# The last FFN of a diffusion backbone: a first pair of eight direct products per weight, and another order of w2's seven products

## The chip, the cores and the metric

The kernel runs on one core of a Trainium2 chip. The metric is the device time of one execution in microseconds. A core has five instruction streams that matter here: TensorE (PE, matrix products into eight PSUM banks), VectorE (DVE), ScalarE (ACT), GpSimd (POOL), and SyncE (SP), which in this kernel issues the DMA transfers. Each stream runs its instructions in order.

## The reference, cut to what matters

The model has two layers; each ends with a SwiGLU FFN on 1024 latent tokens of width 1024. All that follows plays in the FFN of the last layer and the final norm:

```
h   = rms_norm(x, norm2_g) * (1 + ax2) + sx2
x   = x + gx2 * ((silu(h @ w1) * (h @ w3)) @ w2)
out = rms_norm(x, final_norm)
```

The hidden width is 22 blocks of 128, handled as 11 pairs of blocks.

## The kernel before

**Precision.** Every operand is split into a high and a low part (fp32r): ACT copies the high part (`split`, L177), DVE subtracts it to get the low part (L43). A product of two 128-wide operands is then three matmuls: high x high, high x low, low x high.

**Seven products.** Each product with a weight is a 2x2 block scheme with seven block products in place of eight (Strassen-Winograd). The two halves of 512 tokens are one index, the halves of the model width the other. `ops[0..6]` are the seven token operands: 0 and 5 are the two width halves of token half 0 (`b11`, `b21`), 1 and 3 come from half 1 (1 is `b12 - b11`, 3 is `b22`), and 2, 4, 6 are further sums. `WSet.get(i)` makes weight operand i of a pair: POOL builds a sum of raw weight blocks (into `fsum` or in place), ACT and DVE split it into a slot of `ring`. One product is 12 matmuls of 128x512 (L1412), into one of the PSUM banks A, B, C of its weight. `step(i)` in `Gate.seven` issues product i and what takes its result out of the bank; `gate` forms silu(h w1) * (h w3) of four blocks and seven sums of them, which go to DRAM (`g_d`) as the token operands of w2.

**The first pair.** Ahead of it runs the out-projection of the layer (`out_proj`, matmuls L215 to L217), half 0 and then half 1. Half 0 is normed and split as soon as it is there. Half 1's norm goes PE column (`pcol`, L160), DVE (`rsv`, L154), POOL (`rs`), PE broadcast (`prow`, L169), DVE (`nrm`, L46); only then can operands 1, 2, 3, 4, 6 be formed. In the first pair all four engines keep a hand-written order (L1969 and on): products 0 and 5 of w1 and w3, which need half 0 alone, then 1, 2, 3, 4, 6 of both. Five of the seven weight operands of the next pair's w1 (`n1`) are made here.

**Pairs 1 to 10** are ordered by a scheduler, products 0 to 6 of each weight in program order; DVE, ACT and POOL follow.

**w2.** Seven products i in `W2_ORDER`, each a loop over 11 steps j: `w2_op` loads and makes the weight operand, `x_op` loads the token operand from `g_d` and splits it, and four PSUM banks b take three matmuls each (L2053 to L2055). PE and SP keep the written order here, the others do not. Four banks are used over products 0 and 5, four others over 1 and 3, four over 2, 4 and 6. Behind the 11 steps of a product the results leave the banks by `put` (DVE, L46, into `xo`), partly with a saved copy of product 0 (`p1s`). `stat` squares a finished column on ACT into one of two `fsum` buffers and adds it up on POOL for the final norm; `col` and `scale` norm a finished half, and `scale` ends with its stores to `out` (L2088). The layer's input `xs_d` comes back into `xo` by loads at odd j of products 0, 5, 1, 3. The products 1, 3 and 2 share weight sums, kept in `stash`.

Of the kernel before, what the change touches and what calls it, by code (L numbers as in the profile page):

```python
# [8 lines left out]
F32 = mybir.dt.float32  # L9
# [26 lines left out]
def build(tc, a):  # L36
# [1307 lines left out]
    class WSet:  # L1344
        def __init__(self, f, n, j, place=False):
            self.f, self.s, self.place = f, [], place
            self.r = f.pre.pop(0) if f.pre else [f.raw(a[n][f.l, 2 * j + i]) for i in range(2)]
            self.w = {}

        def get(self, i):  # L1350
            if i not in self.w:
# [6 lines left out]
                elif i == 2:  # L1358
                    src = self.s[0] if self.place else self.f.fsum()
# [16 lines left out]
    class Gate:  # L1376
# [16 lines left out]
        def wset(self, n, j, place=False):  # L1393
            return WSet(self, n, j, place)

        def seven(self, w, o, done):
# [11 lines left out]
            def prod(n, i, start):  # L1408
                (wh, wl), (xh, xl) = w.get(i), self.ops[i]
# [6 lines left out]
            def step(i):  # L1416
# [3 lines left out]
                elif i == 1:  # L1420
                    v = prod("C", 1, True)
                    S.copy(out=tmp("p5"), in_=v)
                elif i == 2:
                    tt(V, o[0], st["p1"], prod("B", 2, True), ALU.add)
                elif i == 3:
                    tt(V, o[0], o[0], prod("C", 3, False), ALU.add)
# [10 lines left out]
            return step  # L1437

        def steps(self, store, ws):
# [5 lines left out]
            def gate(i, v):  # L1445
# [9 lines left out]
                if i == 2:  # L1455
                    store(5, b21)
                    tt(G, c[3], b21, c[4], ALU.subtract)
                    store(6, c[3])
                elif {0, 1, 3} <= have:
# [3 lines left out]
                    store(2, c[4])  # L1463

# [6 lines left out]
            return self.seven(ws[0], [s[:, i] for i in (1, 2, 3)], silu), self.seven(ws[1], c, gate), late  # L1471

        def pair(self, j, store, ws=(None, None), mid=None):
# [3 lines left out]
            for u in range(2):  # L1477
                for i in range(7):
                    ws[u].get(i)
                for i in range(7):  # L1480
# [4 lines left out]
    W2_ORDER = (0, 5, 1, 3, 2, 4, 6)  # L1485

    def w2_op(l, i, j, raw, fsum, slot, stash):
# [3 lines left out]
        if i == 2:  # L1491
            split(S, wh, wl, t)
            return wh, wl
        r = raw().rearrange("p (f k) c -> p f (k c)", f=2)
        if i in (0, 5, 6):
            q, c = {0: (0, 0), 5: (1, 0), 6: (1, 512)}[i]
            Q.dma_start(out=r[:, 0], in_=w[:, q, c:c + 512])
            src = r[:, 0]
        elif i == 1:
            Q.dma_start(out=r, in_=w[:, :, 512:])  # L1500
            tt(G, t, r[:, 0], r[:, 1], ALU.add)
            src = t
# [4 lines left out]
        else:  # L1507
            Q.dma_start(out=r, in_=w[:, :, 0:512])
            tt(G, t, t, r[:, 0], ALU.subtract)
            src = r[:, 1]  # L1510
            tt(G, src, src, t, ALU.subtract)
# [407 lines left out]
    first = [part(flat[i], 4)[:, c:c + 1024] for i in range(2) for c in (0, 1024)]  # L1919
# [11 lines left out]
    w1, w3 = [f.wset(n, 0, True) for n in ("ffn_w1", "ffn_w3")]  # L1931
    for w in (w1, w3):
        for i in (0, 5):
            w.get(i)
# [3 lines left out]
    for _ in range(2):  # L1938
        wr.tile([P, 4, P], F32, name="fsum", bufs=2)
    ring = [wr.tile([P, 1024], F32R, name=f"ring{i}") for i in range(4)]  # L1940
    for n, w, b in (("s", 2048, 1), ("pu", 512, 4)):
# [5 lines left out]
    t1, t3, late = f.steps(store(0), (w1, w3))  # L1947
    sh = lambda k: mod[:, 1, 3, 0, k:k + 1]

    def nrm(k):  # L1950
        stt(x[1][:, k], x[1][:, k], mod[:, 1, 4, 0, k:k + 1], pr, ALU.mult, ALU.mult)

    def bias(k):
        S.activation(out=x[1][:, k], in_=x[1][:, k], func=AF.Identity, bias=sh(k))

    def cutk(i, src, u, e=V):
        h, l, v = ops[i][0][:, kk[u]], ops[i][1][:, kk[u]], src[:, kk[u]]
        S.copy(out=h, in_=v)
        return lambda: tt(e, l, v, h.bitcast(F32), ALU.subtract)

    def subk(out, in0, in1):
# [306 lines left out]
```

## Time and profile before

| what | us |
|---|---|
| median of 3 runs | 3294.45 (3291.11 to 3295.41) |
| the profiled execution | 3295.82, its span 3294.0 |
| end of the out-projection, start of the first pair's own stretch | 2556.26 |
| first matmul of pair 1 | 2621.86 |
| first matmul of w2 | 3015.37 |
| last matmul of w2 | 3280.27 |

The span is the time from the first to the last instruction that the profiler saw; the execution's own time is 1.8 us longer. All later times are counted from the start of the span. PE is busy for 3057.9 us, 93% of the span, and its mean granted clock is 0.969 of full speed. The two stretches that the change touches begin at 2550: the first pair until about 2635, and w2 with the final norm from 3015 on.

### The profile page before, as it was taken

Reading aid. Unit: us, or ns where it says so; the run is one execution under the profiler, and the core shown is the slowest. Engines: PE = TensorE matmul, PEld = TensorE weight load, DVE = VectorE, ACT = ScalarE, POOL = GpSimd, SP = SyncE. Lnnn points to the kernel's source line nnn. Section 1 sums busy time; section 2 is a strip of 40 time slices with the busy share of each in tenths; the row PEclk is TensorE's granted clock in tenths of the full one; section 3 lists DMA queues with packets and bytes.
Section 4 is the critical chain, followed back from the end, with each engine's and each line's share of the span. In section 5 each row is a group of like instructions: output and inputs, shape, how many; then the busy total and the mean of one; then the engine's idle time right before and its main releaser. Section 6 shows DMA issues by size and latency. Waiting matters only on the chain.

```text
span 3294.0 us, 49782 instructions
## 1 busy us (share of the span) xinstructions
PE 3057.9 (93%) x18986; PEld 2730.4 (83%) x18986; DVE 2139.5 (65%) x3438; ACT 1323.2 (40%) x2649; POOL 1364.3 (41%) x1253
## 2 busy tenths in 40 slices
PE   6977999979999998999998999998999799999997
PEld 4656777769999998999998999998987588887775
DVE  5764777774876778777777466664355665555664
ACT  3324777553533334443434333321224333333433
POOL 1556881022744445454443332332122565552532
PEclk8998999989999999999999999999999899999998
DMA  7873001445433331433331101111125133324744
GB/s 243 267 169 101 16 19 46 123 132 198 148 109 116 110 109 65 160 111 108 109 114 72 46 27 38 39 43 45 39 78 201 45 115 99 105 97 155 261 155 139
DMA packets 167752, 360.21 MB, mean 109 GB/s; under 512 B 29513, under 2 KB 61913, under 8 KB 166745
## 3 DMA queue, kind: packets, MB, share of 16 engines
q1 hardware_dynamic: 167513, 357.03, 33.5%
q8 instruction: 149, 2.44, 0.3%
q14 instruction: 90, 0.74, 0.1%
HBM read 290.87 MB, written 66.10 MB: 108 GB/s over the span
## 4 chain that ended last, share of the span: by engine, by line
PE 66%; DVE 10%; issue 5%; ACT 4%; POOL 3%; DMA 2%; SPq 0%; POOLq 0%; DVEq 0%; ACTq 0%
PE psf L1412 11%; PE psf L1258 11%; PE psu L215 4%; PE psu L216 4%; PE psu L217 4%; PE psf L215 2%; PE psf L216 2%; PE psf L217 2%; PE pso L2053 2%; PE pso L2054 2%; PE pso L2055 2%; PE pso L217 2%; PE pso L216 2%; PE pso L215 2%; PE psl L1731 2%
## 5 line engine op out<-in xcount | busy, mean ns | idle before, releaser
L1412 PE MATMUL psf<-mix,ring 128*128 128x512 f32 x1320 | 321.6, 399 | 21.3 <-ACT ring L177 9.4
L215 PE MATMUL psu<-mh,wh 128*128 128x384 f32 (+1 forms) x1024 | 327.6, 320 | 1.7 <-ACT qr L1609 1.2
L217 PE MATMUL psu<-mh,wl 128*128 128x384 f32 (+1 forms) x1024 | 324.1, 317 | 0.0
L216 PE MATMUL psu<-ml,wh 128*128 128x384 f32 (+1 forms) x1024 | 323.4, 316 | 0.0
L1412 PEld LDWEIGHTS psf<-mix,ring 128*128 128x128 f32 x1320 | 251.2, 191 | 83.4 <-ACT ring L177 11.3
L215 PEld LDWEIGHTS psu<-mh,wh 128*128 128x128 f32 x1024 | 195.0, 190 | 2.2 <-ACT qr L1609 1.4
L43 POOL TENSOR_TENSOR fsum<-fraw,fsum 128x512 f32<-128x512 f32 x66 | 107.8, 1634 | 214.4 <-DVE ml L43 106.2
L216 PEld LDWEIGHTS psu<-ml,wh 128*128 128x128 f32 x1024 | 194.9, 190 | 0.1
L217 PEld LDWEIGHTS psu<-mh,wl 128*128 128x128 f32 x1024 | 194.7, 190 | 0.1
L46 DVE SCALAR_TENSOR_TENSOR x<-psf,mod,x 128x384 f32<-128x384 f32 (+1 forms) x352 | 175.4, 540 | 25.0 <-PE psf L217 21.1
L43 POOL TENSOR_TENSOR fsum<-fraw 128x512 f32<-128x512 f32 x77 | 117.2, 1523 | 106.2 <-DMA fraw<-ffn_w 94.3
L43 DVE TENSOR_TENSOR ml<-fraw,ml 128x512 fp32r<-128x512 f32 x132 | 124.3, 942 | 38.6 <-ACT ml L177 36.6
L43 POOL TENSOR_TENSOR s<-s,c 128x320 f32<-128x320 f32 x60 | 73.9, 1232 | 175.8 <-DVE c L43 167.1
L1258 PE MATMUL psf<-opx,mh 128*128 128x320 f32 x792 | 134.0, 310 | 0.8 <-DVE mh L43 0.8
L43 DVE TENSOR_TENSOR wx<-pT,wx 128x512 fp32r<-128x512 f32 x168 | 113.0, 681 | 33.4 <-ACT wx L836 33.4
L1258 PE MATMUL psf<-opx,ml 128*128 128x320 f32 x792 | 128.8, 310 | 0.2 <-DVE ml L43 0.2
L43 DVE TENSOR_TENSOR wl<-wraw,wh 128x1024 fp32r<-128x1024 f32 x61 | 90.4, 1481 | 59.2 <-ACT wh L177 49.1
L829 ACT ACTIVATE pt<-pss,st 128x512 f32<-128x512 f32 (+1 forms) x208 | 123.3, 603 | 13.4 <-DVE st L817 11.4
L43 POOL TENSOR_TENSOR acc<-acc,sq 128x384 f32<-128x384 f32 (+2 forms) x57 | 71.6, 1263 | 134.1 <-ACT sq L1129 120.2
L177 ACT CAST ml<-fraw 128x512 fp32r<-128x512 f32 x132 | 81.7, 619 | 113.0 <-PE psf L216 35.0
L43 POOL TENSOR_TENSOR xa<-xa,tot 128x1280 f32<-128x1280 f32 x24 | 87.2, 3632 | 90.4 <-ACT ku L1723 76.0
L1258 PEld LDWEIGHTS psf<-opx,mh 128*128 128x128 f32 x792 | 120.0, 188 | 3.5 <-issue 2.5
(457 smaller groups left out, 9213.5 us busy)
## 6 DMA issues: line engine op xcount, KB each, us to landing
fraw<-ffn_w SPq DMA_DIRECT2D x209, 512.0 KB
early<-w_mod SPq DMA_DIRECT2D x48, 512.0 KB
fraw<-w_mod SPq DMA_DIRECT2D x48, 512.0 KB
opx<-g_d SPq DMA_DIRECT2D x77, 256.0 KB
wraw<-w_odd SPq DMA_DIRECT2D x36, 512.0 KB
g_d<-s SPq DMA_DIRECT2D x44, 256.0 KB
g_d<-c SPq DMA_DIRECT2D x33, 256.0 KB
fraw<-ffn_w SPq DMA_DIRECT2D x33, 256.0 KB
```

What stands on the lines that cost most here:

```text
L43: return e.tensor_tensor(out=out, in0=in0, in1=in1, op=op)
L46: return V.scalar_tensor_tensor(out=out, in0=in0, scalar=scalar, in1=in1, op0=op0, op1=op1)
L177: S.copy(out=hi, in_=src)
L215: PE.matmul(ps, wh, xh, start=start, stop=False)
L216: PE.matmul(ps, wh, xl, start=False, stop=False)
L217: PE.matmul(ps, wl, xh, start=False, stop=stop)
L829: S.activation(out=o, in_=ps, func=AF.Exp, bias=st, accum_out=dd)
L1258: PE.matmul(ps, u[:, k], v[:, k], start=start and k == 0 and j == 0, stop=(k == 3 and j == 2), skip_group_check=True)
L1412: PE.matmul(ps(n), u[:, k], v[:, k], start=start and k == 0 and j == 0, stop=(k == 3 and j == 2), skip_group_check=True)
L1731: PE.matmul(ps[:, c], ku[:, c], qu, start=True, stop=True)
L2053: PE.matmul(o, wh, h, start=first, stop=False, skip_group_check=True)
L2054: PE.matmul(o, wh, l, start=False, stop=False, skip_group_check=True)
```

## The change

**First pair.** In place of seven products on sums, each weight makes eight direct products: its four raw blocks (weights 0, 5, 7, 6, with no sums) with operands 0 and 5 for half 0 and with operands 1 and 3 for half 1 (operand 1 is `b12 - b11`, so the half-1 banks hold a difference to half 0, and `eight` adds the half-0 result back). The eight products of half 0 of both weights come first. Operands 2, 4, 6 are formed for pair 1 only. PE alone keeps a hand-written order. The next pair's weights are no longer made there; `first`, w1's four slots, moves to the place of operand 2.

**Pairs 1 to 10** issue products 0, 5, 1, 3, 2, 4, 6 in place of 0 to 6. The stores of the last pair's seven sums are kept back and issued on SP behind w2's loads of step 3.

**w2.** Order 0, 2, 5, 4, 1, 6, 3; products 2, 4, 6 use one group of four banks, 0, 5, 1, 3 the other, so that the groups alternate. Product 2 loads three raw blocks a step and makes the stash with two POOL sums; 1 and 3 load one block and make one sum each. The loads of `xs_d` stand at the last four steps of products 0, 2, 5, 4. The stores of the half that is done first (now half 0) are issued behind all loads of the last product.

```diff
@@ class WSet, class Gate
-                    src = {0: a11, 5: a12, 6: a22}[i]
+                    src = {0: a11, 5: a12, 6: a22, 7: a21}[i]
...
+            def eight(h, f, half):
+                n, r = "AB"[f] if h == 0 else "CD"[f], ((0, 5), (7, 6))[f]
+                if half == 0:
+                    v = prod(n, r[0], True, (0, 1)[h])
+                    if h == 0:
+                        S.copy(out=tmp("q%d" % f), in_=v)
+                    return
+                v = prod(n, r[1], False, (5, 3)[h])
+                if h == 0:
+                    done(2 * f, v)
+                else:
+                    q = st["q%d" % f]
+                    d = o[2 * f] if o else q
+                    tt(V, d, q, v, ALU.add)
+                    done(2 * f + 1, d)
+            return eight if direct else step
...
-                for i in range(7):
-                    (t1, t3)[u](i)
+                for i in ORDER:
+                    (t1, t3)[u](i)
...
-    W2_ORDER = (0, 5, 1, 3, 2, 4, 6)
+    ORDER = (0, 5, 1, 3, 2, 4, 6)
+    W2_ORDER = (0, 2, 5, 4, 1, 6, 3)
@@ def w2_op
+            if i == 1:
+                tt(G, src, src, t, ALU.add)
+            elif i == 3:
+                tt(G, src, src, t, ALU.subtract)
...
+            r2 = rr()
+            Q.dma_start(out=r.rearrange("p f c -> p (f c)"), in_=w[:, 0])
+            Q.dma_start(out=r2[:, 0], in_=w[:, 1, 512:])
+            tt(G, t, r[:, 1], r[:, 0], ALU.subtract)
+            tt(G, t, t, r2[:, 0], ALU.add)
+            src = t
@@ the first pair
-    first = [part(flat[i], 4)[:, c:c + 1024] for i in range(2) for c in (0, 1024)]
+    first = [part(flat[i], 1)[:, c:c + 1024] for i in range(2) for c in (0, 1024)]
...
+    with tc.manual_schedule(engines={PE.engine}):
+        t1(0, 0, 0)
         acc.col(0, pp)
+        t1(0, 0, 1)
         pr = acc.bc(0, pp)
+        for k in range(KT):
+            h = x[1][:, k]
+            stt(h, h, mod[:, 1, 4, 0, k:k + 1], pr, ALU.mult, ALU.mult)
+            if k < 4:
+                stt(h, h, sh(k), b11[:, k], ALU.add, ALU.subtract)
+            else:
+                S.activation(out=h, in_=h, func=AF.Identity, bias=sh(k))
+            if k == 3:
+                cut(1, b12)
+        cut(3, b22)
...
+        t1(0, 1, 0)
+        t1(0, 1, 1)
+        for i in range(2):
+            for v in range(2):
+                t3(0, i, v)
+        sub(b12, b22, b12)
+        for i in range(2):
+            for v in range(2):
+                t1(1, i, v)
+        cut(2, b12)
+        sub(b11, b12, b11)
+        cut(4, b11)
+        sub(b12, b21, b12)
+        cut(6, b12)
...
+        for i in range(2):
+            for v in range(2):
+                t3(1, i, v)
...
+    kept = []
+    f.pair(NF // 2 - 1, lambda i, v: kept.append((i, v)))
@@ w2
+    PUT = {2: (1,), 5: (0,), 4: (3,), 1: (3,), 6: (2,), 3: (1,)}
+    P1 = {2: 1, 4: 3, 1: 2}
+    LOAD = {0: 1, 2: 0, 5: 3, 4: 2}
+    DONE = {5: 0, 1: 3, 6: 2}
...
+            ps = psb if i in (2, 4, 6) else psa
...
+                if i == 0 and j == 3:
+                    for u, v in kept:
+                        Q.dma_start(out=g_d[u, NJ - 1], in_=v)
+                if i in LOAD and j >= NJ - 4:
+                    d, t, _ = xv(LOAD[i], j - NJ + 4, 0, 0)
+                    Q.dma_start(out=xo[:, d, t:t + 512], in_=xs_d[t // 512, :, d, 0:512])
+                if not last or j < NJ - NT:
                     for b in range(4):
+                        mms(ps[b], *wx[j], b, 0, 512, new and j == 0, j == NJ - 1)
+                if last and j == 2:
+                    rs = col(0, 512)
+                if last and j == 4:
+                    out = scale(0, 512, rs)
+            if last:
+                out()
+                break
```

Three places in the instruction order. First PE, in the first pair, behind the broadcast of half 1's norm (`opx` holds operands 0 and 5 of half 0 and later of others, `mix` those of half 1; ring numbers name the weight slots, and the products before these rows are the same in both). Before:

```order
L1412 MATMUL psf<-opx,mix 128x512 x24
L1412 MATMUL psf<-mix,ring_24697 128x512 x12
L1412 MATMUL psf<-mix,ring_24698 128x512 x12
L1412 MATMUL psf<-mix,ring_24699 128x512 x12
L1412 MATMUL psf<-mix,ring_24697 128x512 x12
L1412 MATMUL psf<-mix,ring_24700 128x512 x12
L1412 MATMUL psf<-mix,ring_24698 128x512 x12
L1412 MATMUL psf<-mix,ring_24699 128x512 x12
L1412 MATMUL psf<-mix,ring_24700 128x512 x12
L1412 MATMUL psf<-mix,ring_24697 128x512 x12
```

And after:

```order
L1412 MATMUL psf<-opx,mix 128x512 x24
L1412 MATMUL psf<-opx,ring_24695 128x512 x12
L1412 MATMUL psf<-opx,ring_24696 128x512 x12
L1412 MATMUL psf<-opx,ring_24697 128x512 x12
L1412 MATMUL psf<-opx,ring_24698 128x512 x12
L1412 MATMUL psf<-mix 128x512 x48
L1412 MATMUL psf<-mix,ring_24695 128x512 x12
L1412 MATMUL psf<-mix,ring_24696 128x512 x12
L1412 MATMUL psf<-mix,ring_24697 128x512 x12
L1412 MATMUL psf<-mix,ring_24698 128x512 x12
```

Behind the broadcast 24 matmuls on half 0 followed before, then the products with half 1; now 72 on half 0 follow, then 96 on half 1.

Second SP, around the start of w2 (`g_d<-s` and `g_d<-c` are stores of the last pair's sums, `fraw<-ffn_w` and `opx<-g_d` the loads of a step's weight and token operand, `xo<-xs_d` the loads of the layer's input). Before:

```order
L2047 DMA opx<-g_d 128x512
L1497 DMA fraw<-ffn_w 128x512
L2047 DMA opx<-g_d 128x512
L1946 DMA g_d<-s 128x512 x2
L1946 DMA g_d<-c 128x512
L1946 DMA g_d<-s 128x512 x2
L1946 DMA g_d<-c 128x512 x2
L2110 DMA xo<-xs_d 128x512
L1497 DMA fraw<-ffn_w 128x512
L2047 DMA opx<-g_d 128x512
L1497 DMA fraw<-ffn_w 128x512
L2047 DMA opx<-g_d 128x512
```

And after:

```order
L1515 DMA fraw<-ffn_w 128x512
L2027 DMA opx<-g_d 128x512
L1515 DMA fraw<-ffn_w 128x512
L2027 DMA opx<-g_d 128x512
L2092 DMA g_d<-s 128x512 x2
L2092 DMA g_d<-c 128x512
L2092 DMA g_d<-s 128x512
L2092 DMA g_d<-c 128x512
L2092 DMA g_d<-s 128x512
L2092 DMA g_d<-c 128x512
L1515 DMA fraw<-ffn_w 128x512
L2027 DMA opx<-g_d 128x512
```

The seven stores stood behind two steps of loads and stand behind four now, and the first `xo` load, which came with step 1, follows at step 7.

Third POOL, in w2, where product 4 makes its weight sums (`fsum<-fraw`) and a finished column is added up (`sum...` or `acc...<-...,fsum`). Before, at the end of product 2:

```order
L43 TENSOR_TENSOR stash<-stash,fraw 128x512
L43 TENSOR_TENSOR fraw<-fraw,stash 128x512
L43 TENSOR_TENSOR sum_27638<-sum_27638,fsum 128x512 x2
L43 TENSOR_TENSOR fsum<-fraw 128x512
L43 TENSOR_TENSOR sum_27638<-sum_27638,fsum 128x512
L43 TENSOR_TENSOR fsum<-fraw 128x512 x10
L43 TENSOR_TENSOR sum_27638<-sum_27638,fsum 128x512 x4
```

And after, at the end of product 5:

```order
L43 TENSOR_TENSOR stash<-fraw 128x512
L43 TENSOR_TENSOR stash<-stash,fraw 128x512
L43 TENSOR_TENSOR acc_27628<-acc_27628,fsum 128x512 x3
L43 TENSOR_TENSOR fsum<-fraw 128x512 x11
L43 TENSOR_TENSOR fraw<-fraw,stash 128x512 x11
L43 TENSOR_TENSOR sum_27629<-sum_27629,fsum 128x512 x3
```

One of the sums of product 4 stood between the adds; now all three adds stand ahead of the eleven sums.

## Rows read from the trace of the kernel before

**Rows 1.** PE's waits, 2556 to 2660: engine, tile, line, releaser; total, times, longest us.

```profile
PE psf L1412 <- ACT ring L177: 9.4, 4, 4.7
PE psf L1412 <- ACT mix L1958: 6.3, 2, 6.1
```

**Rows 2.** Timeline of PE: start, duration, line, tile<-inputs, shape, count, [idle before <- releaser].

```profile
2530.38 0.39 PE L215 MATMUL pso<-mix,wh 128*128 128x512 f32 x1
...
2550.10 0.39 PE L215 MATMUL pso<-mix,wh 128*128 128x512 f32 x1
...
3036.98 0.39 PE L2053 MATMUL pso<-opx,mix 128*128 128x512 f32 x1
...
3046.78 0.39 PE L2053 MATMUL pso<-opx,mix 128*128 128x512 f32 x1
```

**Rows 3.** Windows: length, busy us (instructions) of each engine, granted clock, DMA share, GB/s.

```profile
2580.00:2590.00 10.00, 5.86 (x12) 3.76 (x12) 5.47 (x6) 4.40 (x5) 4.40 (x3) 0.51 0.00 0
...
2650.00:2800.00 150.00, 150.00 (x655) 122.58 (x654) 86.16 (x104) 50.21 (x87) 83.92 (x56) 1.00 0.32 108
...
3030.00:3040.00 10.00, 10.00 (x36) 7.93 (x35) 7.70 (x13) 7.02 (x12) 0.00 (x0) 0.79 1.05 386
```

**Rows 4.** Timeline of PE, end of pair 10 and w2.

```profile
3012.51 3.02 PE L1412 MATMUL psf<-mix,ring 128*128 128x512 f32 x12 [0.55 <-DVE c L43]
3015.37 0.39 PE L2053 MATMUL pso<-opx,ring 128*128 128x512 f32 x1
...
3028.63 0.79 PE L2053 MATMUL pso<-opx,ring 128*128 128x512 f32 x1 [7.16 <-ACT opx L177]
...
3198.42 0.80 PE L2053 MATMUL pso<-opx,mix 128*128 128x512 f32 x1 [4.41 <-ACT mix L177]
...
3257.81 0.79 PE L2053 MATMUL pso<-opx,mix 128*128 128x512 f32 x1 [12.32 <-ACT opx L177]
...
3280.27 0.28 PE L2055 MATMUL pso<-opx,mix 128*128 128x256 f32 x1
```

**Rows 5.** PE's waits for DVE's evictions, 3010 to 3294.

```profile
PE pso L2053 <- DVE xo L46: 9.8, 4, 4.0
```

**Rows 6.** Timeline of PE, first pair.

```profile
2556.26 2.26 PE L1412 MATMUL psf<-opx,mix 128*128 128x512 f32 x9
...
2559.76 3.03 PE L1412 MATMUL psf<-opx,mix 128*128 128x512 f32 x12
...
2563.45 3.05 PE L1412 MATMUL psf<-opx,mix 128*128 128x512 f32 x12
```

**Rows 7.** Timeline of DVE, first pair: a weight split, a normalisation, splits.

```profile
2560.02 0.68 DVE L43 TENSOR_TENSOR ring<-fsum,ring 128x512 fp32r<-128x512 f32 x1
2563.73 0.75 DVE L46 SCALAR_TENSOR_TENSOR x<-x,mod,prow 128x512 f32<-128x512 f32 x1 [3.03 <-PE prow L169]
...
2568.09 1.23 DVE L43 TENSOR_TENSOR mix<-x,mix 128x1024 fp32r<-128x1024 f32 x1
...
2579.93 2.28 DVE L43 TENSOR_TENSOR x<-x 128x1024 f32<-128x1024 f32 x1
```

**Rows 8.** Timeline of POOL, the norm's column.

```profile
2560.18 1.40 POOL L43 TENSOR_TENSOR rs<-rsv,nhalf 128x4 f32<-128x4 f32 x1 [5.73 <-DVE rsv L154]
```

**Rows 9.** Timeline of SP: DMA issues at w2's start and in its last product.

```profile
3013.08 1.89 SPq L1946 DMA_DIRECT2D g_d<-s  x2
...
3023.00 0.42 SPq L1497 DMA_DIRECT2D fraw<-ffn_w  x1
...
3247.64 3.49 SPq L2088 DMA_DIRECT2D out<-xo  x4
```

**Rows 10.** Timeline of POOL, product 3: first of the two sums of two steps.

```profile
3107.92 1.74 POOL L43 TENSOR_TENSOR stash<-stash,fraw 128x512 f32<-128x512 f32 x1
...
3111.33 1.74 POOL L43 TENSOR_TENSOR stash<-stash,fraw 128x512 f32<-128x512 f32 x1
```

**Rows 11.** Timeline of POOL, end of product 2: the first add of squares.

```profile
3192.13 1.30 POOL L43 TENSOR_TENSOR sum<-sum,fsum 128x512 f32<-128x512 f32 x1 [40.47 <-ACT fsum L2070]
```

More of the change, by code (lines that the diff above doesn't have):

```diff
@@ L1358, in get @@
                 elif i == 2:
[L1359 removed]
+                    src = self.f.fsum()
                     tt(G, src, self.s[0], a11, ALU.subtract)
@@ L1436, in step, with steps @@
                     done(2, o[1])
-            return step
-        def steps(self, store, ws):
+            def eight(h, f, half):
[14 more added lines that the diff above has]
+            return eight if direct else step
+        def steps(self, store, ws, direct=False):
             nh, have = self.nh, set()
@@ L1470, in late @@
                 c.extend(ct[:, i] for i in range(5))
-            return self.seven(ws[0], [s[:, i] for i in (1, 2, 3)], silu), self.seven(ws[1], c, gate), late
+            return (self.seven(ws[0], [s[:, i] for i in (1, 2, 3)], silu, direct),
+                    self.seven(ws[1], None if direct else c, gate, direct), late)
         def pair(self, j, store, ws=(None, None), mid=None):
@@ L1946, in build @@
     store = lambda j: lambda i, v: Q.dma_start(out=g_d[i, j], in_=v)
-    t1, t3, late = f.steps(store(0), (w1, w3))
+    t1, t3, late = f.steps(store(0), (w1, w3), True)
     sh = lambda k: mod[:, 1, 3, 0, k:k + 1]
[L1950 to L1959, printed above, removed]
@@ L2097, in build @@
                 ps = [bank() for _ in range(4)]
-            if i == 1:
-                stash = big.tile([P, KT * T], F32, name="stash", tag="H0")
-                wslots[0] = itertools.cycle(ring + [flat[0][:, c:c + 1024] for c in range(0, 10240, 1024)])
-            new, end = i in (0, 1, 2), i in (5, 3, 6)
-            u = DEST.get(i, 0)
+                if i == 2:
+                    psb, stash = ps, big.tile([P, KT * T], F32, name="stash", tag="H0")
+                else:
+                    psa = ps
@@ L2103, in build @@
+            ps = psb if i in (2, 4, 6) else psa
+            new, last = i in (0, 1, 2), i == W2_ORDER[-1]
             wx = [None] * NJ
             for j in range(NJ):
-                wx[j] = w2_op(1, i, j, fraw, fsum, next(wslots[0]), stash), x_op(i, j)
-                if i in (0, 5, 1, 3) and j % 2 and j < 8:
-                    q, d = divmod({0: 0, 5: 3, 1: 1, 3: 2}[i], 2)
-                    d = 4 * q + j // 2
-                    t = {0: 0, 5: 1, 1: 1, 3: 0}[i]
-                    Q.dma_start(out=xo[:, d, 512 * t:512 * t + 512], in_=xs_d[t, :, d, 0:512])
@@ new lines, in build @@
+                if last and j == 2:
[5 more added lines that the diff above has]
+                break
+            for b in range(4):
+                if i == 0:
+                    S.copy(out=p1s[:, b], in_=ps[b])
+                for u in PUT.get(i, ()):
+                    put(ps[b], *xv(u, b, 0, 512))
+                if i in P1:
+                    put(p1s[:, b], *xv(P1[i], b, 0, 512))
+                if i in DONE:
+                    stat(xv(DONE[i], b, 0, 0)[0], 512 * (DONE[i] % 2), 512)
@@ new lines, in build @@
+        for t0, n in (0, 256), (256, 256):
+            for b in range(4):
+                for j in range(NJ - NT, NJ):
+                    mms(ps[b][:, t0:t0 + n], *wx[j], b, t0, n, False, j == NJ - 1)
+                put(ps[b][:, t0:t0 + n], *xv(1, b, t0, n))
+                stat(b, 512 + t0, n, V if t0 else G)
+                if t0 and b == 1:
+                    rs = col(512, 256)
+                if t0 and b == 3:
+                    scale(512, 256, rs)()
+        scale(768, 256, col(768, 256))()
```

167 lines of the change are left out of this document (37 added, 130 removed).

## The prediction

> **What bounds the kernel now.** I read the waits of TensorE (PE) first, in the two stretches that the diff touches, then its timeline there, then the engines that end the waits, then SP's queue. In the first pair of the last FFN PE waits mostly for ScalarE's (ACT) copies, of half 1's operands (mix) and of weights (ring) [rows 1], and VectorE (DVE) and GpSimd (POOL) make what ACT copies. Where nothing is missing PE starts a 128x512 matmul every 0.2267 us: 87 of them lie between the two rows of [rows 2] (19.72 us). In w2 it is 42 matmuls in 9.80 us, 0.2333 us each. Pairs 1 to 10 leave PE no idle time: in 2650 to 2800 it is busy 150.00 of 150.00 at full granted clock [rows 3]. So a microsecond saved in front of them is a microsecond of the end, and one saved in w2 too, as long as the tail behind the last w2 matmul keeps its length.
>
> How much the two stretches lose now:
> - Pairs 1 to 10 are 10 x 14 x 12 = 1680 matmuls, 380.9 us at 0.2267. w2 starts at 3015.37 [rows 4], so without any loss pair 1 would have had to start at 2634.5. That is the effective end of the first pair.
> - w2 is 7 x 11 x 12 = 924 matmuls' worth, 215.6 us at 0.2333. From 3015.37 to the last matmul at 3280.27 it takes 264.9 [rows 4]. With about 3 us for the norm's small matmuls, some 46 us are lost. PE's waits of 7.16, 4.41 and 12.32 us [rows 4] and four for DVE's evictions, 9.8 us [rows 5], are 34 of them; the other 12 are matmuls at the lower clock behind them (granted 0.51 of full speed behind the like wait in the first pair [rows 3]).
>
> **The first pair.** Sixteen products for fourteen: 24 matmuls more, 5.4 us of PE. In return eight of them (96 matmuls, for four before) need half 0 alone, which is there before the out-projection ends. 3 of the 192 run ahead of 2556.26, so 189 x 0.2267 = 42.8 us. The norm's two small groups stand between the products as before and cost 1.46 us (2558.30, the end of the nine matmuls, to 2559.76) and 0.97 us (2562.48 to 2563.45) [rows 6]. PE alone would end at 2556.26 + 42.8 + 2.4 = 2601.5. Three things can be late:
> - Operands 1 and 3. The eight products of half 0 end at 2556.26 + 2.4 + 93 x 0.2267 = 2579.8. DVE's new order has eight normalisations and four subtractions of 0.75 us from 2563.73 on [rows 7], so until 2572.7, then three to four splits of 1.23 us alone, up to 2.28 when POOL runs beside them [rows 7]. Operand 1 is ready at 2575.2 to 2577.3, in time; operand 3, one product later (2582.5), at 2578.9 to 2584.1. Loss 0 to 1.6.
> - The norm's column rs on POOL. It started at 2560.18 [rows 8]; now three sums for pair 1 (1.3 us each) stand ahead of it, behind a load. If the load is there by 2556 rs moves to about 2560.5, which the next twelve matmuls cover; each us of a later load is a us of the first pair. Loss 0 to 3.
> - Pair 1's weights. w1's first slots now lie in operand 2's place, so operand 2 is split only when the w1 products end (2579.8 + 48 x 0.2267 = 2590.7), and ring2 lies where the half-1 input still is. Behind 2590.7 stand four to five DVE steps of 1.23 to 2.28: 2596 to 2602, with pair 1's splits behind, against 2601.5. Loss 0 to 8.
>
> I take 3 us for the three together: effective end 2604.5, gain 2634.5 - 2604.5 = **30 us**, between 21 and 33.
>
> The Trainium skill, "SBUF — State Buffer", section "Who interferes with whom", says that a DVE instruction with two SBUF inputs and a GpSimd instruction that reads SBUF exclude each other for the whole instruction. It speaks against the second POOL sum per step, below: The trace agrees for a single split, 1.23 us alone and 2.28 beside POOL [rows 7]. Taken strictly, product 2 would take 3.96 us a step by it where POOL and DVE did with 3.41 before [rows 10]; the sum would be 3242.
>
> **Pairs 1 to 10.** The order 0,5,1,3,2,4,6 puts three products of bank B next to each other in program order, each waiting for DVE's add of the one before. In the instruction order the other weight's products lie between them, 27 to 50 matmuls at the places I looked at. The only neighbours are at the end of pair 10, as before, where the wait is 0.55 us [rows 4]. I take 0.
>
> **w2.** Four losses of before and what is in their place:
> - Its start. Before, seven stores of the last pair, each waiting for its product, stand on SP ahead of the third step's loads: first store 3013.08, next weight load 3023.00 [rows 9], PE waits 7.16 us [rows 4] and is slow after. Now four steps of loads (4 x 2.8 us of PE work, until 3026.6 on the old time axis) come first, and the x_s loads have moved behind step 7. The last pair's last product ends with the start of w2 and the stores' data are there some us later, so the fifth step's load follows in time or nearly. Loss 1 (0 to 4); was about 10.
> - The bank waits. Products now alternate between two groups of four banks, so eviction has a whole product (30.8 us) of time: the four waits of [rows 5] go (about 16 us with the slow clock). Their price: product 2 makes its weights with two POOL sums a step. POOL with two sums a step ran at 3.41 us (3107.92 to 3111.33 [rows 10]) against PE's 2.8. Eleven steps are 37.5 us; POOL can start some 8 us before product 2 does, as loads of product 0 free buffers. 37.5 - 8 - 28 (PE's start of the eleventh step) = 1.5, and 512 + 256 KB of weights and 256 KB of x a step are 1 MB, 2.7 us at the 386 GB/s of [rows 3]. Raw buffers hold two steps only, so a slow landing adds. Loss 4 (0 to 10).
> - Product 4. Its weight sums use the two fsum buffers that the squares of the finished half-column use as well; before, PE waited 4.41 us there [rows 4]. Now three squares and adds of product 5, 1.30 us each [rows 11], stand ahead of the first sum on POOL. From the end of product 5: 0.2 until the first square is there, three adds, a sum of 1.6, a copy of 0.6 make 6.4 us, with 2.4 at the lower clock 9. Was 7. Loss 9 (6 to 12).
> - The last product. Before, the finished half's four stores held SP (the last wait and their issue end at 3247.64 + 3.49 = 3251.1 [rows 9], loads only then), PE waited 12.32 us [rows 4]: about 15 with the slow clock. Now stores are issued behind all loads: 0. The norm of that half comes in step 2 of the last product, and its adds on POOL alternate with that product's sums: loss 2 (0 to 4).
>
> 1 + 4 + 9 + 2 = 16 in place of 46: gain **30 us**, between 18 and 40. The tail behind the last matmul is the same code on the other half: 0.
>
> **The sum** is made against the profiled execution, 3295.82 us (span 3294.0): 3295.8 - 30 - 30 = 3235.8. It lies 1.4 us above the median, so I say 3235.
>
> **Rivals.**
> - The first pair is bound by its elementwise work. Only PE keeps a hand-written order there; before, all four engines had one. If all splits take 2.28 us and rs is late by 3, pair 1's weights come at 2612 to 2615 and the lower clock adds a few: gain 18 for 30, 3248. For it: DVE was busy most of the time there, and PE's present waits are all of this kind [rows 1]. Against it: half 0's products cover 2557 to 2580. 0.15.
> - w2 gives back more. If POOL and DVE shut each other out in product 2, a step takes its two POOL sums and two DVE splits one behind the other, 2 x 1.30 + 2 x 0.68 = 3.96 us [rows 7, 11]; 0.55 over 3.41 is 6 us in eleven steps; and if product 4 starts as late as the old last product did (12.32 us for 6.4), 6 more: 3248. For it: one split did take 2.28 for 1.23; against it: the 3.41 was measured with the same four steps. 0.12; both rivals at once, 3260, 0.04.
> - Slower: bank B. If PE reaches products 4 and 6 before DVE's add has freed their bank, in pairs 1 to 10 there are 2 waits x 2 weights x 10 pairs = 40 on a path that has no idle time now. At the 0.55 us of [rows 4] they cost 22; a DVE add caught behind a split of 2.28 makes it 2.4 us and 96 in all, 3332. It decides from 1.5 us each, where it eats the 60. Against it the interleaving above. 0.04.
> - The change does less than it says: the interleaving of loads keeps the start of w2 as it is (SP still held by a store that waits), +9, 3245. In the instruction order the loads do stand ahead. 0.05, inside the range.
>
> **Chances.** Forecast 0.60, first-pair rival 0.15, w2 rival 0.12, late start 0.05, both 0.04, slower 0.04. What a measurement of this kernel can tell from no change is about 0.2%, 6.6 us. Faster 0.94, within 0.02 (a mix of bank waits and lost gains), slower 0.04. The range goes from full gains (33 and 40: 3222, two less for the profile) to both rivals with a little over: 3220 to 3262.
>
> **What would show it.** In the new profile: the first w2 matmul some 30 us earlier, at 2985; waits for ACT mix in the first pair gone, waits for ACT ring under 4 us in all; no wait for DVE xo in w2; one wait of 6 us for ACT's copy in product 4; none in the last product. Wrong it would be if PE were under 10.00 busy in pairs 1 to 10 (bank B), if waits of over 8 us for ACT ring stood around the start of pair 1, or if product 2 showed a wait in every step.

## The result, and the profile after

The changed kernel (called after below) takes 3241.5 us (median of 4 runs, 3237.1 to 3254.1), the kernel before 3292.8 in the same runs: a ratio of 0.985, 95% interval 0.982 to 0.988. The forecast was 3235, with 3220 to 3262 as its range. The profiled execution of after has a span of 3242.6 us, 51.4 less than before.

Where they went is read from three stretches of PE's timeline. What runs ahead of them is the same code in every kernel here, but begins the last FFN up to 11.5 us earlier or later from run to run; so lengths are compared, not times of day: from the nine matmuls at the end of the out-projection to the first matmul of w2; from there to the last matmul of w2; and the tail to the end of the span.

| | first pair and pairs 1 to 10 | w2 | tail |
|---|---|---|---|
| before | 459.1 | 264.9 | 13.7 |
| after | 436.7 | 236.7 | 12.7 |
| forecast (before less its terms) | 429 | 235 | 13.7 |

PE's timeline of after in the first pair (start, duration, line, tile<-inputs, shape, count, idle before and its releaser):

```profile
2556.50 2.26 PE L1412 MATMUL psf<-opx,mix 128*128 128x512 f32 x9
...
2567.43 3.07 PE L1412 MATMUL psf<-opx,mix 128*128 128x512 f32 x12 [0.68 <-ACT pu L1443]
...
2574.85 5.86 PE L1412 MATMUL psf<-opx,ring 128*128 128x512 f32 x24 [1.55 <-ACT pu L1443]
2581.39 3.07 PE L1412 MATMUL psf<-opx,ring 128*128 128x512 f32 x12 [0.68 <-ACT pu L1443]
2584.30 11.06 PE L1412 MATMUL psf<-mix 128*128 128x512 f32 x48
2595.20 11.04 PE L1412 MATMUL psf<-mix,ring 128*128 128x512 f32 x48
2606.08 0.62 PE L1412 MATMUL psf<-opx,ring 128*128 128x512 f32 x2
```

Half 1's operands come in time: the 48 matmuls on `mix` start without a wait, where [rows 1] had 6.3 us of waits for ACT's copies of them, and the 9.4 us for its copies of weights have gone too. Three waits for ACT at L1443 stand there instead, each for the copy of a half-0 result out of its PSUM bank. The first of them stood in the kernel before as well, in PE's timeline at the same place; the other two are new:

```profile
2567.17 3.07 PE L1412 MATMUL psf<-opx,mix 128*128 128x512 f32 x12 [0.68 <-ACT pu L1419]
```

Pair 1 starts 49.6 us behind the nine matmuls.

Its w2, same view:

```profile
2990.28 3.04 PE L1412 MATMUL psf<-mix,ring 128*128 128x512 f32 x12 [0.78 <-DVE c L43]
2993.15 0.39 PE L2033 MATMUL pso<-opx,ring 128*128 128x512 f32 x1
...
3049.02 0.50 PE L2035 MATMUL pso<-opx,mix 128*128 128x512 f32 x1 [0.90 <-DVE mix L43]
...
3094.60 0.80 PE L2033 MATMUL pso<-opx,mix 128*128 128x512 f32 x1 [6.01 <-ACT mix L177]
...
3202.36 1.87 PE L160 MATMUL pcol<-onec,acc 128*128 128x2 f32 x8 [4.37 <-POOL acc L43]
...
3229.87 0.28 PE L2035 MATMUL pso<-opx,mix 128*128 128x256 f32 x1
```

The waits of [rows 4] at the start (7.16) and in the last product (12.32) and the four of [rows 5] have gone. Product 4 waits 6.01 us, product 2 in four places 1.8 us together (the largest is shown), and a wait of 4.37 us has come in front of the norm's column product (L160), which stands in PE's order behind step 2 of the last product.

### The profile page after: what moved, and what is told of

Read it like the earlier page. It is cut to its first block, busy times and chain, and to the rows that moved or that the text cites. A ratio compares the mean times of both kernels' runs of the same rounds, so it can differ in the third digit from the quotient of the medians.

```text
span 3242.6 us, 49888 instructions
## 1 busy us (share of the span) xinstructions
PE 3045.4 (94%) x19010; PEld 2727.4 (84%) x19010; DVE 2113.4 (65%) x3431; ACT 1321.8 (41%) x2643; POOL 1352.8 (42%) x1251
## 4 chain that ended last, share of the span: by engine, by line
PE 67%; DVE 8%; issue 5%; POOL 4%; ACT 4%; DMA 2%; SPq 0%; POOLq 0%; ACTq 0%; DVEq 0%
PE psf L1412 13%; PE psf L1258 11%; PE psu L215 5%; PE psu L216 5%; PE psu L217 5%; PE psf L215 2%; PE psf L216 2%; PE psf L217 2%; PE pso L217 2%; PE pso L216 2%; PE pso L215 2%; PE psl L1751 2%; PE pso L2033 2%; PE pso L2035 2%; PE pso L2034 2%
## 5 line engine op out<-in xcount | busy, mean ns | idle before, releaser
L1412 PE MATMUL psf<-mix,ring 128*128 128x512 f32 x1248 | 295.7, 392 | 0.8 <-DVE c L43 0.8
L1412 PEld LDWEIGHTS psf<-mix,ring 128*128 128x128 f32 x1248 | 234.4, 188 | 53.2 <-DVE c L43 1.2
L43 POOL TENSOR_TENSOR fsum<-fraw,fsum 128x512 f32<-128x512 f32 x64 | 99.7, 1558 | 234.1 <-DVE ml L43 105.3
L43 POOL TENSOR_TENSOR fsum<-fraw 128x512 f32<-128x512 f32 x75 | 108.1, 1442 | 130.8 <-DMA fraw<-ffn_w 99.7
L1412 PE MATMUL psf<-opx,ring 128*128 128x512 f32 x528 | 131.4, 393 | 2.2 <-ACT pu L1443 2.2
L829 ACT ACTIVATE pt<-pss,st 128x512 f32<-128x512 f32 (+1 forms) x208 | 123.5, 604 | 13.5 <-DVE st L817 11.5
```

What stands on the lines that cost most here:

```text
L43: return e.tensor_tensor(out=out, in0=in0, in1=in1, op=op)
L829: S.activation(out=o, in_=ps, func=AF.Exp, bias=st, accum_out=dd)
L1412: PE.matmul(ps(n), u[:, k], v[:, k], start=start and k == 0 and j == 0, stop=(k == 3 and j == 2), skip_group_check=True)
```

## What the experiments asked

Three losses in after had a suspected cause: the copies at L1443, the 6.01 us at product 4, and the 4.37 us. Parts of the change were taken back: w2 as a whole, the places of two sets of stores and of the loads of the layer's input, and the alternation of the bank groups. In what follows a stretch is one of the three lengths above.

## The first pair alone

w2 is the old one here; the first pair and the order of products in pairs 1 to 10 are the new ones.

```diff
-    W2_ORDER = (0, 2, 5, 4, 1, 6, 3)
+    W2_ORDER = (0, 5, 1, 3, 2, 4, 6)
...
-    f.pair(NF // 2 - 1, lambda i, v: kept.append((i, v)))
+    f.pair(NF // 2 - 1, store(NF // 2 - 1))
```

(w2_op and the loops of w2 as in the kernel before.)

> The new first pair and the new order of products in pairs 1 to 10, with w2 as it was before. Theory: the first pair is worth 22 us and w2 the rest, and the two are independent: w2 starts near 2993 as in the changed kernel and takes the old 265 us from there to its last matmul; time 22 us under the kernel before, ratio 0.993. Rival: part of the gain of the first pair was won at the cost of work pushed into w2 (or the reverse); then w2's length moves by 4 us or more from 265.

Measured: a ratio to the kernel before of 0.9935 (0.9921 to 0.995), 3270.8 us. The stretches are 436.6, 264.3 and 13.2. w2 has its old length and its old waits, PE's timeline:

```profile
3004.63 0.80 PE L2033 MATMUL pso<-opx,ring 128*128 128x512 f32 x1 [7.83 <-ACT opx L177]
...
3233.01 0.80 PE L2033 MATMUL pso<-opx,mix 128*128 128x512 f32 x1 [12.44 <-ACT opx L177]
```

The two halves of the change are independent, as expected: the first pair is worth 22 us, w2 the other 28. The new order of products in the pairs has no part in it: the 1344 matmuls of pairs 2 to 9 take 308.6 us in after and 308.8 before.

## The copies out of a shared bank

```diff
         t1(0, 0, 0)
         acc.col(0, pp)
-        t1(0, 0, 1)
+        t1(0, 1, 0)
...
-        t1(0, 1, 0)
+        t1(0, 0, 1)
         t1(0, 1, 1)
-        for i in range(2):
-            for v in range(2):
+        for v in range(2):
+            for i in range(2):
                 t3(0, i, v)
```

> The first pair's half-0 products in the order 0, 7, 5, 6 of each weight, so that the two products that share a PSUM bank no longer follow each other. Theory: the three waits for ACT's copy of the half-0 result (0.7, 1.6 and 0.7 us) come from that neighbourhood and vanish; pair 1 starts 2.9 to 3.5 us earlier against the end of the out-projection (46.1 to 46.7 us behind the nine matmuls, in place of 49.6), and the end moves by as much, some 3 us. Rival: ACT is late there in itself, behind the splits of half 1's operands; then the waits move to the second copies and the sum stays within 0.7 of 2.9 us.

Measured, PE's timeline (one execution; its time is 3240.1 us):

```profile
2554.69 2.26 PE L1412 MATMUL psf<-opx,mix 128*128 128x512 f32 x9
...
2600.55 0.62 PE L1412 MATMUL psf<-opx,ring 128*128 128x512 f32 x2
```

No wait stands between them; pair 1 starts 45.9 us behind the nine matmuls, 3.7 us earlier than in after, a little more than the waits' 2.9 since each had some tenths of refilling behind it. The stretch is 432.9 for 436.7. In after, the product that adds to a bank came right behind the one whose result ACT had to copy out of it first: 0.7 us when ACT is free (a copy takes 0.6), 1.55 when it was behind three splits. With a product of another bank between them there is nothing to wait for. w2, whose code is the same, came out 0.7 us longer than in after (237.5 for 236.7), so the net is 3.0 us, as expected; 0.7 is also a measure of what w2 differs by from one execution to the next.

## The start of w2: stores or loads

The change moved two things on SP at the start of w2: the last pair's stores, and the loads of the layer's input (`xo<-xs_d`). First the stores alone go back into the pair:

```diff
     kept = []
-    f.pair(NF // 2 - 1, lambda i, v: kept.append((i, v)))
+    f.pair(NF // 2 - 1, store(NF // 2 - 1))
```

> Only the place of the last pair's seven stores goes back: issued within the pair, ahead of w2's third or so step of loads. Theory: SP is held by them again, PE waits some 7 us for ACT's copy of a token operand soon after the start of w2, with 2.4 us at the lower clock behind it: 7 to 10 us slower than the changed kernel. Rival: the x_s loads, which stood at the odd steps before and now stand behind step 7, were what held SP; then the wait stays under 3 us.

Measured: no wait at the start of w2 at all; stretches 438.3, 232.9 and 12.2, in sum 2.7 us shorter than after (w2 3.8 and the tail 0.5 shorter, the end of pair 10 with 1.4 us more of waits). But the edit didn't bring the stores early, as SP's timeline of this run shows:

```profile
2979.82 0.38 SPq L1515 DMA_DIRECT2D fraw<-ffn_w  x1
...
2984.36 0.42 SPq L2027 DMA_DIRECT2D opx<-g_d  x1
2993.68 0.32 SPq L1963 DMA_DIRECT2D g_d<-s  x1
...
2998.14 1.70 SPq L1963 DMA_DIRECT2D g_d<-c  x2
3001.65 0.32 SPq L2095 DMA_DIRECT2D xo<-xs_d  x1
```

and of after:

```profile
2972.04 0.42 SPq L2027 DMA_DIRECT2D opx<-g_d  x1
2981.97 10.75 SPq L2092 DMA_DIRECT2D g_d<-s  x2
...
2998.65 0.40 SPq L1515 DMA_DIRECT2D fraw<-ffn_w  x1
```

Left to the scheduler, six of the seven stores went out behind the loads of eight steps, just ahead of the first load of `xs_d` behind step 7. That is later than in after, where the stores that are kept behind step 3 hold SP from 2972 to 2998 with only four steps loaded. So the run doesn't test the theory; it shows what the stores cost behind step 3. What they delay is not the start but product 2: its first weight sum on POOL starts at 3016.35 in after, 23.2 us behind the start of w2, and at 3014.15 here, 19.8 behind it, and its four waits are gone. So the second suspect went back as well:

```diff
-                if i in LOAD and j >= NJ - 4:
-                    d, t, _ = xv(LOAD[i], j - NJ + 4, 0, 0)
+                if i in LOAD and j % 2 and j < 8:
+                    d, t, _ = xv(LOAD[i], j // 2, 0, 0)
```

(on top of the edit before.)

> As the run with the last pair's stores early, and besides the loads of the layer's input go back to the odd steps 1, 3, 5, 7 of products 0, 2, 5, 4. Theory, formed on that run: what held w2's start in the kernel before was not the stores but the first of these loads at step 1: its target lies in memory that the last pair gives free only when its sums are stored, and SP waits there with all later loads behind it. Then a wait of 6 to 8 us for ACT's copy of a token operand stands again in the third or fourth step of w2, with slow clock behind it: 8 to 11 us over the run with early stores alone. Rival: the eight token slots and the four raw buffers set how far SP runs ahead; then the wait stays under 2 us.

Measured: w2 243.6 us, 10.7 more than in the run before; time 3252.5. PE's timeline, then SP's:

```profile
3007.74 0.80 PE L2033 MATMUL pso<-opx,ring 128*128 128x512 f32 x1 [7.73 <-ACT opx L177]
```

```profile
2971.20 0.34 SPq L2027 DMA_DIRECT2D opx<-g_d  x1
2983.06 10.76 SPq L1963 DMA_DIRECT2D g_d<-s  x2
...
3001.47 0.32 SPq L2095 DMA_DIRECT2D xo<-xs_d  x1
3001.84 0.42 SPq L1515 DMA_DIRECT2D fraw<-ffn_w  x1
```

The old wait is back, at its old size and in the third step. The order on SP is fixed in w2, and `xo` lies where the last pair's ring and sums lay, so the stores have to stand ahead of its first load. With that load at step 1, two steps are loaded ahead of the stores; SP then stands in the stores, which wait for their sums until 2999.65, the load follows 1.8 us later, and the operands of the third step come late. What goes with the start, then, is how many steps of loads stand ahead of the stores: two in the kernel before and here (waits of 7.16 and 7.73 us), four in after and eight in the run before this one (none). To move the `xs_d` loads is enough to remove the 7.16 us of [rows 4], since the scheduler then issues the stores late by itself. That the load rather than the stores held SP, as this theory has it, is not shown: SP waits in the stores, and stores that stand early with the loads moved were not run.

With that known, the stores kept behind step 6, still ahead of the first `xs_d` load:

```diff
-                if i == 0 and j == 3:
+                if i == 0 and j == 6:
                     for u, v in kept:
```

> The last pair's stores are kept behind step 6 of product 0 in place of step 3, still ahead of the first load of the layer's input; all else as in the changed kernel. Theory: the kept stores hold SP for some 12 us at step 4 while it could fetch w2's operands, which makes product 2's weight sums start late; at step 6 they hold nothing that is due: w2 3 to 4 us shorter than in the changed kernel (236.7), no wait in product 2, and no longer wait at the end of pair 10 (0.8 us) than there. Rival: the stores must land before product 0's last step and product 2's loads follow them, so later stores only move the crowd: product 2 waits 2 us or more.

Measured: stretches 437.3, 233.5 and 12.8; w2 is 3.2 us shorter, without a wait in product 2. Seven steps are loaded ahead of the stores. Pair 10's end waits 1.17 us for DVE in two places, 0.4 more than in after, and the first stretch is 0.7 longer, so the net is 2.5 us. The theory holds but for that.

## Product 4 and the two fsum buffers

```diff
-            sq = fsum()[:, :n]
+            sq = wr.tile([P, 512], F32, name="pu", bufs=4)[:, :n]
             S.activation(out=sq, in_=xk, func=AF.Square)
```

> The squares for the final norm go to the four pu buffers, which are free in w2, in place of the two buffers that product 4's weight sums use. Theory: the wait of 6.0 us at the start of product 4 is the price of sharing these buffers; with their own the first six sums are made ahead, the wait goes (under 1 us), with it the 2.4 us of slow clock: w2 some 8 us shorter. Rival: the start of product 4 waits for DVE or the loads as well; then 2 us or more stay, under another name.

In after, timelines of POOL and ACT at the start of product 4:

```profile
3088.73 3.95 POOL L43 TENSOR_TENSOR acc<-acc,fsum 128x512 f32<-128x512 f32 x3 [35.23 <-ACT fsum L2050]
3092.63 2.49 POOL L43 TENSOR_TENSOR fsum<-fraw 128x512 f32<-128x512 f32 x2
```

```profile
3093.93 0.62 ACT L177 CAST mix<-fsum 128x512 fp32r<-128x512 f32 x1 [3.27 <-POOL fsum L43]
```

POOL had been idle for 35 us, product 4's raw weights could have been summed, and the first sum waits for three adds because its buffer holds a square. With the squares elsewhere the first six sums come ahead of the adds, product 4 starts without a wait, and w2 takes 229.8 us for 236.7. The tail grew from 12.7 to 13.9: with the buffers free, the scheduler put five scalings on DVE ahead of the last add of a square, and the last column product waits 3.01 us in place of 1.19:

```profile
3220.33 0.98 PE L160 MATMUL pcol<-onec,sum 128*128 128x2 f32 x4 [3.01 <-DVE sum L43]
```

Net 5.7 us (one execution, 3232.4 us). The theory holds: the wait went whole, and w2 gave 6.9 us where some 8 were expected.

## The norm's column in the last product

```diff
-                if last and j == 2:
+                if last and j == 5:
                     rs = col(0, 512)
-                if last and j == 4:
+                if last and j == 7:
                     out = scale(0, 512, rs)
```

> The norm's column product of the finished half stands behind step 5 of the last product in place of step 2, its broadcast behind step 7 in place of 4. Theory: PE waited 4.4 us there only because POOL's adds of squares stand between that product's weight sums; three steps (8.4 us) later they are done, the wait goes, and so does the stretch at the lower clock behind it (granted 0.66 in ten us): last matmul of w2 6 to 7 us earlier, the tail behind it (12.7 us) as long as before. Rival: the later norm runs into the tail, since its scaling takes DVE, POOL and ACT and its stores share the DMA queues with the last loads: the tail grows by 3 us or more and less than half of the gain is left.

In after POOL alternates the last product's weight sums with the adds of squares, and the last add ends just when PE is let go (3202.36); its timeline:

```profile
3197.24 1.72 POOL L43 TENSOR_TENSOR acc<-acc,fsum 128x512 f32<-128x512 f32 x1
3198.92 1.71 POOL L43 TENSOR_TENSOR fraw<-fraw,stash 128x512 f32<-128x512 f32 x1
3200.60 1.71 POOL L43 TENSOR_TENSOR acc<-acc,fsum 128x512 f32<-128x512 f32 x1
```

Measured with the later column: that wait is gone, w2 takes 232.6 us, 4.1 less, and the tail is 12.7 as before. 2.05 us came back at another place, PE's timeline:

```profile
3220.16 0.38 PE L2033 MATMUL pso<-opx,mix 128*128 128x256 f32 x1 [0.45 <-DVE xo L46]
...
3224.52 0.61 PE L160 MATMUL pcol<-onec,sum 128*128 128x2 f32 x4 [2.05 <-POOL sum L43]
```

POOL's scaling of the finished half, three steps later, now stands ahead of the adds that the third quarter's column needs. The gain was 4 where 6 to 7 were expected; the theory's cause was right, and the rival's collision is real but lies ahead of the tail.

## The stores of the finished half

```diff
                 if last and j == 4:
                     out = scale(0, 512, rs)
+                    out()
             if last:
-                out()
                 break
```

> Only the place of the stores of the half that is done first goes back: issued behind step 4 of the last product, among its loads. Theory: SP waits for the scaled columns and holds back the last loads: PE waits 8 to 13 us behind step 6 or 7 and the end comes 10 to 15 us later than in the changed kernel. Rival: the loads were ahead far enough here, since the norm stands two steps later than in the kernel before; then under 4 us.

Measured: w2 246.6 us, 9.8 more; time 3251.7. SP's timeline and PE's:

```profile
3205.47 3.49 SPq L2067 DMA_DIRECT2D out<-xo  x4
3209.05 0.97 SPq L1515 DMA_DIRECT2D fraw<-ffn_w  x1
```

```profile
3215.76 0.80 PE L2033 MATMUL pso<-opx,ring 128*128 128x512 f32 x1 [12.44 <-ACT ring L177]
```

This is the wait of [rows 4] in the last product, at its old size of 12.3; the loads go out only behind the stores. The wait of 4.4 us in front of the column product doesn't stand in this run: with the loads held, POOL has no weight sums to put between its adds, and takes all four at once:

```profile
3186.98 5.40 POOL L43 TENSOR_TENSOR acc<-acc,fsum 128x512 f32<-128x512 f32 x4 [5.55 <-ACT fsum L2050]
```

So the net is less than the wait and its slow clock, and just under the 10 to 15 us expected. Here it is the place of the stores alone.

## Neighbours on the same banks

```diff
-    W2_ORDER = (0, 2, 5, 4, 1, 6, 3)
+    W2_ORDER = (0, 5, 2, 4, 1, 6, 3)
...
-    LOAD = {0: 1, 2: 0, 5: 3, 4: 2}
+    LOAD = {0: 0, 5: 1, 2: 3, 4: 2}
```

> w2 in the order 0, 5, 2, 4, 1, 6, 3: products 0 and 5 and products 2 and 4 share their four banks and follow each other; all else as in the changed kernel. Theory: without a product between them the next one waits for DVE to empty the banks: four waits of some 10 us in all in front of product 4, 5 us of lower clock, and about 1 us in front of product 5, while the 6.0 us for the shared buffers in product 4 go (no squares there): 6 to 10 us slower than the changed kernel. Rival: DVE empties four banks in time once POOL has one sum a step; then the swap is even or faster by 6 to 8.

Measured: a ratio to the kernel before of 0.9846 (0.9826 to 0.9866), the same as after's 0.9852. Stretches 436.7, 234.0 and 12.3. PE's timeline:

```profile
3089.79 0.76 PE L2033 MATMUL pso<-opx,mix 128*128 128x512 f32 x1 [5.06 <-DVE xo L46]
...
3093.28 0.80 PE L2033 MATMUL pso<-opx,mix 128*128 128x512 f32 x1 [0.26 <-DVE xo L46]
```

The 6 to 10 us that the theory expected to lose were not lost; it was the rival's even swap. The neighbours 2 and 4 cost 5.3 us of wait, half of the 9.8 of [rows 5] (products 1 and 3 there); products 0 and 5, also neighbours, cost no wait. The swap saves the 6.0 us of product 4, whose sums no longer stand behind squares, and product 2's waits, since POOL has a product more of time for its two sums a step. So the alternation between 2 and 4, as it stands, gained nothing: what it saves at the banks it paid at the fsum buffers. Whether it gains once the squares have buffers of their own was not run.

## The edits together

First the three edits to the first pair, the column and the squares:

> The three edits together (banks of the first pair apart, later column, squares in buffers of their own). If each wait is a loss by itself on PE's path, the gains add: 3 + 6.5 + 8 = 17.5 us under the changed kernel, a ratio to the kernel before of about 0.980 in place of 0.985, and a profiled span of about 3225. Rival: they hide each other in part (what PE gets earlier it waits for later); then the span stays above 3232.

Measured: 3227.0 us, ratio 0.9796 (0.978 to 0.9812), stretches 432.9, 226.0 and 13.9. By the stretches that is 13.2 us under after, not 17.5: 3.7 + 10.7 - 1.2. Alone the edits gave 3.0, 4.2 and 5.7 net, 12.9 together: the gains add, and what is missing is what two of them gave less than expected. The span of 3225.1 agrees with the expected 3225 only because this run entered the last FFN 4.3 us earlier than after's.

Then with the stores behind step 6, the column behind step 4 and its broadcast behind step 6 (between the two places tried), and only the squares of whole columns in the pu buffers:

```diff
-            sq = fsum()[:, :n]
+            sq = fsum() if n < 512 else wr.tile([P, 512], F32, name="pu", bufs=4)
+            sq = sq[:, :n]
```

> What the runs gave, together: banks of the first pair apart (3.7 us), the stores kept behind step 6 (3 to 4), squares of whole columns in the pu buffers and those of the last quarter-columns in the old ones (6.9, with no longer tail), the finished half's norm column behind step 4 and its broadcast behind step 6 of the last product (4 to 6). If they add: 17 to 20 us under the changed kernel, a ratio to the kernel before of 0.978 to 0.980, profiled span 3222 to 3226. Rival: the waits are linked (the earlier end of one product makes the next one's sums late): a ratio of 0.9815 or more.

Measured: 3224.8 us (3222.7 to 3227.8), ratio 0.9782 (0.9767 to 0.9797), stretches 433.3, 218.2 and 12.8: 21.8 us under after, more than the parts add up to. The single runs of the squares and of the later column still had waits in product 2 (3.3 and 2.9 us), and the second had 2.5 us new in the last product; none of these stands here. PE's timeline, with the only wait between the first and the last matmul of w2:

```profile
2994.97 0.39 PE L2033 MATMUL pso<-opx,ring 128*128 128x512 f32 x1
...
3051.82 0.50 PE L2035 MATMUL pso<-opx,mix 128*128 128x512 f32 x1 [0.23 <-DVE mix L43]
...
3213.21 0.28 PE L2035 MATMUL pso<-opx,mix 128*128 128x256 f32 x1
```

218.2 is 215.6 us of matmuls and the norm's small ones: w2 is bound by PE. This version beats both kernels: its interval of ratios lies under after's.

## Why the prediction was right, and where its terms were off

The range held the time and the direction was right; the gain was 51.4 us in the profiles for 60 forecast. By its steps:

- **First pair, 30 forecast, 22.2 measured** (22.5 by the stretch, less 0.2 that the nine matmuls came later). Two terms failed. The first is the pitch: pairs 1 to 10 were put at 380.9 us, with the 0.2267 us a matmul read in the out-projection, and all other time ahead of w2 was put on the first pair. In after they take 387.07 us (2606.08 to 2993.15, both shown above) with one wait of 0.78 in them, so 0.2299 a matmul. [rows 3] could have told: 150 us at 655 instructions is 0.229. Some 6 us of the loss that I saw in the first pair were time of the pairs themselves and not to be won. The second is the copies: I let the half-0 products run without a wait, and didn't look at what stands between two products on one bank, though the kernel before showed one such wait, 0.68 us at 2567.17. They cost 2.9 us and 0.8 behind them, as the run with the banks apart shows.
- **What could be late there.** None was. rs started at 2560.43 (forecast about 2560.5), operands 1 and 3 were in time, and pair 1's weights too. The 3 us that I allowed went to the copies in their place, so pair 1's start at 2606.08, for 2604.5 forecast, was near by luck.
- **Start of w2, 1 forecast, 0 measured** (w2 as a whole 30 forecast, 28.2 measured). Size and mechanism held: more steps of loads stand ahead of the stores. But of the two moves that I named the one of the `xs_d` loads is enough by itself, and the stores kept behind step 3 cost 2.5 to 2.7 us net, in product 2.
- **Product 2, 4 forecast.** 1.8 us of waits, 3.2 with the gaps in the matmuls around them by the run with the stores at step 6. The waits aren't steady: 1.8 to 2.9 us in the kernels whose w2 is the same up to there. POOL's step was 3.40 us, as forecast from [rows 10], and the start of the sums was late, 23.2 us behind the start of w2 where I had 22.8. The rival of 3.96 us a step did not come. POOL's timeline of after, two steps:

```profile
3018.97 1.75 POOL L43 TENSOR_TENSOR stash<-fraw 128x512 f32<-128x512 f32 x1
...
3022.37 1.74 POOL L43 TENSOR_TENSOR stash<-fraw 128x512 f32<-128x512 f32 x1
```

- **Product 4, 9 forecast.** The wait was 6.01 for 6.4, with the slow clock behind it; 6.9 by the run with the squares apart. Mechanism and size hold.
- **The last product, 2 forecast.** No wait for loads, as forecast. The column product cost 4.37 us of wait for POOL's alternating adds and sums: the right mechanism at twice its size; moving it gave 4.1.
- **The tail, 0 forecast**, gave 1.0.
- **The slower rival** had no support: the end of pair 10 waits 0.78 us for 0.55, and PE is busy throughout the pairs, in after's window:

```profile
2650.00:2800.00 150.00, 150.00 (x655) 122.69 (x654) 75.95 (x102) 50.96 (x87) 76.33 (x54) 1.00 0.32 106
```

- **Slips in the sum.** Operand 3's bounds count five splits where the text says three to four; with four it is ready by 2581.8 at the latest, and the loss is 0. The parts given for product 4 add up to 6.3, not 6.4. The worst losses of w2 add up to 30, which leaves a gain of 16, not 18. None of them moves the forecast.

## What to carry to other kernels

Read the pitch of a stretch from that stretch itself: a pitch 1.4% off was worth more here (5 us) than all the waits of the new first pair. When a queue that runs in order is rearranged, ask for each entry what it waits for, and what has to stand ahead of it; here one load into memory that wasn't free yet brought seven stores forward in the queue, and all loads behind them waited until the stores had their data. And look at the order that was issued, not only at the order that was written: one run here was meant to bring the stores early and brought them late. And two uses of a small buffer pool (squares and weight sums) tie two chains together that have nothing else in common: a free buffer elsewhere was worth more than the reordering around it.

## What the runs showed of the hardware

- The same matmul (128x512, fp32r, three to a block) starts every 0.2267 us in the first pair of after (48 in 10.88 us from 2595.20 to 2606.08), every 0.2299 in the pairs behind it (1680 in 387.07 us less the wait of 0.78) and every 0.2333 in w2 ([rows 2]; the same in after), all at full granted clock and, but for the 0.78, without a wait in the records. What sets the difference wasn't tried and stays open.
- A DVE subtract and a POOL subtract that overlap slow one of the two, and which one depends on who came first. In after's first pair DVE starts at 2577.59 and keeps its 1.22 us, and POOL, starting at 2577.76, takes 3.32 where the same subtract took 2.35 in the kernel before; in the kernel before the DVE operation came second, at 2579.93 behind a POOL sum of 2579.42, and took 2.28 for 1.23 [rows 7]. The Trainium skill says so, "SBUF — State Buffer", section "Who interferes with whom": a DVE instruction with two SBUF inputs contends with a GpSimd one that reads SBUF, and the order of issue decides who blocks. These single cases agree with it. In product 2, where two sums and two splits share a step, all four ran longer than alone, but the step took 3.40 us, less than the 3.96 of their solo times one behind the other.

Timelines of after for the first of these, DVE and POOL:

```profile
2577.59 1.22 DVE L43 TENSOR_TENSOR x<-x,x 128x1024 f32<-128x1024 f32 x1
```

```profile
2577.76 3.32 POOL L43 TENSOR_TENSOR x<-x 128x1024 f32<-128x1024 f32 x1 [15.93 <-DVE mix L43]
```
